# A threshold search over float keys on VectorE, replaced by one over two 16-bit halves on VectorE and ScalarE

## The chip, the cores and the metric

The kernel runs on one core of one Trainium2 chip. The metric is the device time of the whole program in microseconds (us). A core has five engines that work side by side, each on its own queue in order: TensorE (PE in the profile, PEld for its weight loads), VectorE (DVE), ScalarE (ACT), GpSimd (POOL) and SyncE (SP, which issues the DMAs here).

## The reference

One decoder layer over 1,024 tokens of width 1,024: an RWKV-7 mixer and a sparse attention side by side, merged by gates, then a SwiGLU feed-forward network. What matters here is how the sparse attention chooses its keys. An indexer gives each query a score for each earlier key, and the 256 best keys stay:

```python
score = jnp.einsum('bqhs,bqh->bqs', sc, wib) * idx_scale
score = jnp.where(causal, score, -jnp.inf)
_, sel = lax.top_k(score, topk)            # topk = 256
valid = sel <= t[None, :, None]
```

Queries come in eight blocks of 128. Blocks 0 and 1 have at most 256 keys before them and need no choice; block b of 2 to 7 chooses among (b+1) x 128 keys, that is 384 to 1,024. Where scores are equal, the lower index wins. The kernel turns the choice into an additive mask, `bias[b]`: 0 where a key stays, -1e30 where it does not.

## The kernel before

PE works through a list of matmuls in exactly the order in which the program was written; the other engines' queues are ordered by a scheduler at compile time, by program order and by its own idea of when things are ready. What sets PE's order is the pump: `fill` is a queue of generators, and `pump(n)` (L134) takes n matmuls' worth of work from it and puts them into PE's list at that place. So matmuls that depend on nothing urgent (the fill) stand between the steps of a chain that leaves PE free.

The layer's large products are done by `mm3` (L117): weights and activations are each split into a high and a low part, and three products are added, which makes 24 matmuls of 128 x 512 for one column of 128 outputs and one half of the tokens. `weights` (L106) loads a weight tile by SP, ACT copies its high part (L103), DVE subtracts to get the low part (L104). The result in PSUM is emptied by ACT and DVE: L265, L266, L268 and L270 for the rwkv columns, L282 to L286 with L103/L104 or L293/L294 for attention's k and q (rotary embedding), L363 and a transpose (L350, L352) for v, a Tanh on ACT (L376) for the gates.

The order around the change: `norm1` and the indexer's projections; then `fill` is given `proj_rwkv` (14 columns, 672 matmuls) and `proj_qkv` (12 columns, 576 matmuls and some transposes, 1,258 credits with the former), 72 are pumped, and `scores` (L732) computes the indexer scores, 80 pieces with a pump of 2 after each. Then `proj_gates` of half 0 (16 columns, 384 matmuls) joins the queue and `select` (L763) runs. After it the pools of scores and masks' helpers are closed and `rwkv(0)` (L404) runs, in whose fill stand what is left of the gates and then `att0`, the attention of half 0 blended with the other half's gates (748 credits). `rwkv(0)` pumps 806 credits: 403 in each of its two quarters, the first 16 of them ahead of its first matmul (L425, L433). What is still in the queue then runs behind it by `run(*fill)`, before `rwkv(1)` starts.

`select` looks for the 256th largest score of each query bit by bit: in each of 32 steps DVE proposes a bit (L781), counts in each of the six blocks how many scores reach the proposed threshold (L783, one pass with an accumulated sum), compares the count with 256 and keeps the bit or not (L785, L786), and 38 matmuls are pumped. Unsigned integers stand for floats: a mask `mk`, settled after the first step, makes their order that of the scores. The last part (L799 to L810) sets all above the threshold, takes as many ties as are needed by a running sum, and writes the mask.

Of the kernel before, what the change touches and what calls it, by code (L numbers as in the profile page):

```python
# [11 lines left out]
F32 = mybir.dt.float32  # L12
F32R = mybir.dt.float32r
BF16 = mybir.dt.bfloat16
U32 = mybir.dt.uint32
AF = mybir.ActivationFunctionType
ALU = mybir.AluOpType
AX = mybir.AxisListType
# [2 lines left out]
S = 1024  # L21
# [3 lines left out]
TOPK = 256  # L25
C1 = math.exp(-0.5)
NEG = -3.0e38
BIG = 1.0e30
# [17 lines left out]
def block_kernel(ctx: ExitStack, tc: tile.TileContext, ins: dict, outT: bass.AP, stop=None, dbg=None):  # L46
    nc = tc.nc
    V, A, G, T, SY = nc.vector, nc.scalar, nc.gpsimd, nc.tensor, nc.sync
# [47 lines left out]
    def mix():  # L96
        return psM.tile([128, HT], F32, tag="mix", name="mix")
# [33 lines left out]
    fill = deque()  # L131
    credit = [0]

    def pump(n):  # L134

        credit[0] += n
        while credit[0] > 0 and fill:
            try:
                credit[0] -= abs(next(fill[0]))
            except StopIteration:  # L140
                fill.popleft()
        if not fill:
            credit[0] = 0

    def run(*gens):
        for g in gens:
            for _ in g:
                pass
# [31 lines left out]
    def opened(side, name, **kw):  # L180
        stack = ExitStack()
        return stack, stack.enter_context(tc.tile_pool(name=name, bufs=1, side=side, reuse_waits="tile", **kw))
# [59 lines left out]
    def proj(ct, us, out, off=0, between=None):  # L242
        w = weights(ins["w_in"][ct])
        for half, u in enumerate(us):
            if half == 1 and between:
                between()
            ps = acc()
            o = off if half == 0 else 0
            yield from mm3(ps[:, :HT - o], w, u, tok=slice(o, HT))
            out(half, ps)  # L250

    def stage(pool, dt=F32):
        return pool.tile([128, 2, HT], dt, tag="stg", name="stg", bufs=2)

    def proj_rwkv(us, pj):
        for g0, n in ((CT_WA, 1), (CT_GD, 1), (CT_K, 4), (CT_R, 4), (CT_V, 4)):
            for j in range(n):
                ct = g0 + j
                st = stage(pj)
                mu = par[:, P_MU + ct:P_MU + ct + 1]  # L260
                pss = []

                def out(half, ps):
                    s = st[:, half, :]
                    A.activation(s, ps, AF.Copy, scale=omu[:, ct:ct + 1])  # L265
                    V.scalar_tensor_tensor(s[:, 1:], ps[:, :HT - 1], mu, s[:, 1:], op0=ALU.mult, op1=ALU.add)  # L266
                    if half == 0:
                        A.activation(halo[:, ct:ct + 1], ps[:, HT - 1:HT], AF.Copy)  # L268
                    else:
                        V.scalar_tensor_tensor(s[:, 0:1], halo[:, ct:ct + 1], mu, s[:, 0:1],  # L270
                                               op0=ALU.mult, op1=ALU.add)

                yield from proj(ct, us, out)
                SY.dma_start(d_rw[g0][j], st.rearrange("p h t -> p (h t)"))
# [96 lines left out]
    def proj_gates(half, u):  # L371
        for g in range(16):

            def out(_, ps):
                t = tmp()
                A.activation(t, ps, AF.Tanh, scale=0.5)  # L376
                SY.dma_start(d_g[half][g], t)

            yield from proj(CT_GA + g, [u], out)
# [334 lines left out]
    def pieces(n):  # L714

        m = -(-n // 512)
        return [(i * (n // m), n // m) for i in range(m)]
# [11 lines left out]
                V.tensor_scalar(bias[b][:, b * 128:], caus, BIG / 3.0e38, None, op0=ALU.mult)  # L729
        return caus, bias  # L730

    def scores(p, caus):  # L732

        ik = p.tile([128, 2, S], F32R, name="ik")
        for h in range(2):
            for e in range(2):
                SY.dma_start(ik[64 * e:64 * e + 64, :, h * HT:(h + 1) * HT].bitcast(F32),
                             d_ik[h].rearrange("c p t -> p c t"))
        sc = {}
        for b in range(2, 8):  # L740
            n = (b + 1) * 128
            iq = p.tile([128, 8, 128], F32R, tag="iq", name="iq", bufs=2)
            o = (b % 4) * 128
            SY.dma_start(iq.bitcast(F32), d_iq[b // 4][:, :, o:o + 128].rearrange("h p t -> p h t"))
            s = p.tile([128, n], F32, tag=f"sc{b}", name="sc")
            for c, w in pieces(n):
                for h in range(8):
                    ps = mix()
                    for i in range(2):
                        T.matmul(ps[:, :w], iq[:, h, :], ik[:, i, c:c + w], start=i == 0, stop=i == 1)  # L750
                    rl = p.tile([128, 512], F32, tag="rl", name="rl", bufs=3)
                    A.activation(rl[:, :w], ps[:, :w], AF.Relu)
                    if h == 0:
                        V.tensor_scalar(s[:, c:c + w], rl[:, :w], widx[:, b, 0:1], 0.0, op0=ALU.mult, op1=ALU.add)
                    else:
                        V.scalar_tensor_tensor(s[:, c:c + w], rl[:, :w], widx[:, b, h:h + 1], s[:, c:c + w],
                                               op0=ALU.mult, op1=ALU.add)
                    pump(2)
            V.tensor_tensor(s[:, n - 128:n], s[:, n - 128:n], caus, op=ALU.add)
            sc[b] = s  # L760
        return sc

    def select(p, scs, bias):  # L763

        blocks, sc = list(scs), list(scs.values())
        nb, nk = len(blocks), S

        def small(tag, dt=F32):
            return p.tile([128, nb], dt, tag=tag, name=tag)


        Tk = small("Tk", U32)
        V.memset(Tk, 0)
        mk = small("mk", U32)
        V.memset(mk, 0x80000000)
        cnt = small("cnt")
        junk = p.tile([128, nk], BF16, tag="junk", name="junk")
        f = small("f", U32)
        kb = small("kb", U32)
        for bit in range(31, -1, -1):  # L780
            V.scalar_tensor_tensor(f, Tk, 1 << bit, mk, op0=ALU.bitwise_or, op1=ALU.bitwise_xor)  # L781
            for i, s in enumerate(sc):
                V.tensor_scalar(junk[:, :s.shape[1]], s, f.bitcast(F32)[:, i:i + 1], None, op0=ALU.is_ge,  # L783
                                op1=ALU.add, accum_out=cnt[:, i:i + 1])
            V.tensor_scalar(kb, cnt, TOPK - 0.5, float(1 << bit), op0=ALU.is_ge, op1=ALU.mult)  # L785
            V.tensor_tensor(Tk, Tk, kb, op=ALU.bitwise_or)  # L786
            pump(38)
            if bit == 31:

                neg = small("neg")  # L790
                V.tensor_scalar(neg, cnt, TOPK - 0.5, float(0x7fffff00), op0=ALU.is_lt, op1=ALU.mult)
                negu = small("negu", U32)
                V.tensor_copy(negu, neg)
                V.tensor_tensor(mk, mk, negu, op=ALU.bitwise_or)
                V.tensor_scalar(negu, negu, 8, None, op0=ALU.logical_shift_right)
                V.tensor_tensor(mk, mk, negu, op=ALU.bitwise_or)
        V.tensor_tensor(f, Tk, mk, op=ALU.bitwise_xor)
        tau = f.bitcast(F32)
        for i, s in enumerate(sc):  # L799
            n = s.shape[1]  # L800
            t, r = tau[:, i:i + 1], cnt[:, i:i + 1]
            eq = p.tile([128, nk], F32, tag="eq", name="eq")
            V.tensor_scalar(eq[:, :n], s, t, None, op0=ALU.is_equal)
            V.tensor_scalar(junk[:, :n], s, t, None, op0=ALU.is_gt, op1=ALU.add, accum_out=r)
            V.tensor_scalar(r, r, -1.0, TOPK + 0.5, op0=ALU.mult, op1=ALU.add)
            pre = p.tile([128, nk], F32, tag="pre", name="pre")
            V.tensor_tensor_scan(pre[:, :n], eq[:, :n], eq[:, :n], 0.0, op0=ALU.add, op1=ALU.max)
            V.scalar_tensor_tensor(eq[:, :n], pre[:, :n], r, eq[:, :n], op0=ALU.is_le, op1=ALU.mult)
            V.scalar_tensor_tensor(eq[:, :n], s, t, eq[:, :n], op0=ALU.is_gt, op1=ALU.add)
            V.tensor_scalar(bias[blocks[i]], eq[:, :n], BIG, -BIG, op0=ALU.mult, op1=ALU.add)  # L810

    def attend(half, p, bias):
        blocks, nk = blocks_of[half], (half + 1) * HT
# [196 lines left out]
    def chain(*gens):  # L1010
        for g in gens:
            yield from g
# [9 lines left out]
    caus, bias = masks(bp)  # L1022
# [7 lines left out]
    for st, _ in reversed(sx):  # L1030
        st.close()
    ss, sp = opened("right", "se")
    fill.append(chain(proj_rwkv(us, pj), proj_qkv(us, pj, cs)))
    pump(72)
    scs = scores(sp, caus)
    fill.append(proj_gates(0, us[0]))
    select(sp, scs, bias)
    ss.close()
    sc_.close()
    spj.close()  # L1040
# [112 lines left out]
```

## Time and profile before

| what | us |
|---|---|
| median of 3 runs (lowest, highest) | 2025.36 (2018.75, 2028.1) |
| the profiled execution | 2030.08 |
| its span, first to last instruction | 2028.3 |
| PE busy | 1843.1 |
| DVE busy | 1204.7 |
| ACT busy | 736.8 |
| mean granted clock of PE | 0.942 |

The profile shows one execution. "Busy" adds up instructions; PE's matmuls overlap in the pipeline, so their starts say more than their durations. A row of the order in time gives start and duration in us, the engine, the line of the kernel, the operation, and output and input tiles; in brackets stands how long the engine had been idle before it, and what released it. A row by groups gives the count, the summed busy time in us and the mean of one in ns. A row of waits gives the waiting instruction, whom it waited for, us in total, times, and the longest.

### The profile page before, as it was taken

The numbers are of one execution on the slowest core, as the hardware profiler recorded it, in microseconds if no ns is written. First come the engines' busy times: TensorE is split into PE (matmuls) and PEld (weight loads), VectorE is DVE, ScalarE is ACT, GpSimd is POOL, SyncE is SP. The second block draws the span as 40 slices with busy tenths as digits, with TensorE's granted clock in tenths as the row PEclk, the third lists the DMA queues.
The fourth block names the chain that finished last, engine by engine and source line by source line (L and its number), as shares of the span: only waits on it lengthen the run. The fifth ranks groups of instructions, "written<-read, shape, count | busy, mean of one in ns | idle before, by whom it ended". The sixth has DMA issues, their size and how long they took to land. (4 is left out here: it accounts for less than half of the span.)

```text
span 2028.3 us, 26078 instructions
## 1 busy us (share of the span) xinstructions
PE 1843.1 (91%) x10032; PEld 1483.6 (73%) x10032; DVE 1204.7 (59%) x2245; ACT 736.8 (36%) x1220; POOL 37.6 (2%) x22
## 2 busy tenths in 40 slices
PE   3899888778998898989879989999999989999997
PEld 2788666667787676767758868878878868888885
DVE  5679999999264474479477534433347553333334
ACT  4655112452423533533333435542233323222222
POOL 0000000000000000000010000000000000000000
PEclk9899999999997897979869989999999989999998
DMA  4341122332535343246313285414457432533523
GB/s 168 101 133 71 63 75 81 102 122 67 191 104 161 100 115 92 83 137 197 89 51 103 70 218 165 119 50 146 130 174 223 131 116 94 166 105 116 163 84 114
DMA packets 133316, 242.90 MB, mean 120 GB/s; under 512 B 27836, under 2 KB 57152, under 8 KB 133064
## 3 DMA queue, kind: packets, MB, share of 16 engines
q1 hardware_dynamic: 133192, 241.24, 38.9%
q8 instruction: 79, 1.29, 0.3%
q14 instruction: 45, 0.37, 0.1%
HBM read 188.24 MB, written 52.95 MB: 119 GB/s over the span
## 5 line engine op out<-in xcount | busy, mean ns | idle before, releaser
L104 DVE TENSOR_TENSOR wlo<-wst,whi 128x1024 fp32r<-128x1024 f32 (+1 forms) x231 | 278.4, 1206 | 419.4 <-ACT whi L103 229.2
L103 ACT ACTIVATE whi<-wst 128x1024 fp32r<-128x1024 f32 (+1 forms) x231 | 241.2, 1044 | 429.3 <-PE acc L123 394.4
L122 PE MATMUL acc<-zhi,whi 128*128 128x512 f32 x704 | 281.5, 400 | 0.0
L123 PE MATMUL acc<-zlo,whi 128*128 128x512 f32 x704 | 277.6, 394 | 0.0
L783 DVE TENSOR_SCALAR_CACHE_REDUCE junk<-sc,f 128x384 bf16<-128x384 f32 (+2 forms) x192 | 181.4, 945 | 5.5
L122 PE MATMUL acc<-u1hi,whi 128*128 128x512 f32 x376 | 157.9, 420 | 25.0 <-DVE tmp L284 14.0
L127 PE MATMUL acc<-zhi,wlo 128*128 128x512 f32 x704 | 179.2, 394 | 0.0
L122 PE MATMUL acc<-u0hi,whi 128*128 128x512 f32 (+1 forms) x376 | 153.7, 412 | 22.4 <-DVE stg L266 14.8
L122 PEld LDWEIGHTS acc<-zhi,whi 128*128 128x128 f32 x704 | 133.6, 190 | 30.2 <-issue 2.0
L123 PE MATMUL acc<-u1lo,whi 128*128 128x512 f32 x376 | 153.0, 407 | 1.1 <-DVE u1lo L104 0.9
L123 PEld LDWEIGHTS acc<-zlo,whi 128*128 128x128 f32 x704 | 133.6, 190 | 27.8
L127 PEld LDWEIGHTS acc<-zhi,wlo 128*128 128x128 f32 x704 | 130.9, 188 | 29.3 <-issue 1.6
L123 PE MATMUL acc<-u0lo,whi 128*128 128x512 f32 (+1 forms) x376 | 150.7, 404 | 0.9 <-DVE u0lo L104 0.9
L122 PE MATMUL acc<-fhi,whi 128*128 128x512 f32 x352 | 140.5, 399 | 4.1 <-ACT zhi L103 3.9
L123 PE MATMUL acc<-flo,whi 128*128 128x512 f32 x352 | 139.6, 397 | 1.1 <-DVE flo L104 1.1
L122 PEld LDWEIGHTS acc<-u0hi,whi 128*128 128x128 f32 x376 | 75.7, 201 | 45.8 <-DVE stg L266 18.2
L122 PEld LDWEIGHTS acc<-u1hi,whi 128*128 128x128 f32 x376 | 73.7, 196 | 48.3 <-DVE tmp L284 17.5
L127 PE MATMUL acc<-u1hi,wlo 128*128 128x512 f32 x376 | 101.8, 415 | 0.0
L127 PE MATMUL acc<-u0hi,wlo 128*128 128x512 f32 (+1 forms) x376 | 94.5, 394 | 5.4 <-DVE wlo L104 5.4
L127 PE MATMUL acc<-fhi,wlo 128*128 128x512 f32 x352 | 90.6, 396 | 0.0
L123 PEld LDWEIGHTS acc<-u0lo,whi 128*128 128x128 f32 x376 | 75.6, 201 | 17.4 <-DVE u0lo L104 2.5
L127 PEld LDWEIGHTS acc<-u1hi,wlo 128*128 128x128 f32 x376 | 74.4, 201 | 16.5 <-issue 0.3
(223 smaller groups left out, 2887.4 us busy)
## 6 DMA issues: line engine op xcount, KB each, us to landing
wst<-in_w_ffn_in SPq DMA_DIRECT2D x88, 512.0 KB, 3.5
wst<-in_w_in SPq DMA_DIRECT2D x63, 512.0 KB, 3.8
wst<-in_w_fo SPq DMA_DIRECT2D x32, 512.0 KB, 3.6
k<-d_k SPq DMA_DIRECT2D x48, 256.0 KB, 5.4
h<-in_xT SPq DMA_DIRECT2D x32, 256.0 KB, 5.8
d_g<-tmp SPq DMA_DIRECT2D x32, 256.0 KB, 2.2
wst<-in_w_o SPq DMA_DIRECT2D x16, 512.0 KB, 3.5
tmp<-d_g SPq DMA_DIRECT2D x32, 256.0 KB, 3.2
```

The costliest lines, as they stand in the source:

```text
L103: A.activation(hi, x, AF.Copy)
L104: V.tensor_tensor(lo, x, hi.bitcast(F32), op=ALU.subtract)
L122: T.matmul(ps, whi[:, wk + k, :], ahi[:, ak + k, tok], start=k == 0, stop=False)
L123: T.matmul(ps, whi[:, wk + k, :], alo[:, ak + k, tok], start=False, stop=False)
L127: T.matmul(ps, wlo[:, wk + k, :], ahi[:, ak + k, tok], start=False, stop=k == nk - 1)
L783: V.tensor_scalar(junk[:, :s.shape[1]], s, f.bitcast(F32)[:, i:i + 1], None, op0=ALU.is_ge, op1=ALU.add, accum_out=cnt[:, i:i + 1])
```

## The change

The scores are first turned into integers whose order is that of the floats (an arithmetic shift makes a mask of the sign, an xor applies it), and cut into a high half (multiples of 65,536) and a low half (0 to 65,535), each in a tile of its own per block. Two searches of 16 steps follow, the first on the high halves, the second on the low halves of those keys whose high half equals the one found; for this the difference of the high half and the found one is added to the low half, so that all other keys lie out of reach.

In each step the six blocks are counted on two engines: blocks 5, 3 and 2 (768, 512 and 384 keys) by DVE as before, blocks 7, 6 and 4 (1,024, 896 and 640 keys) by ACT, as a sum of `Sign(x + z)`, whose threshold is 2 x 256 - 1 - n. A vector `sgn` of +1 and -1 lets the three small instructions that follow serve both kinds at once. The pumps become 14 after each block's cutting, 18 after each step, 20 between the searches and 22 after each block's mask. The gates of half 0 no longer join the queue before the search: what is left of rwkv and qkv is run out behind it, and only then the gates are queued, for `rwkv(0)`. The scores' tiles stay in one pool, the scoring's other tiles go into a pool that is closed before the search, and the search's tiles take its place.

```diff
-        for bit in range(31, -1, -1):
-            V.scalar_tensor_tensor(f, Tk, 1 << bit, mk, op0=ALU.bitwise_or, op1=ALU.bitwise_xor)
-            for i, s in enumerate(sc):
-                V.tensor_scalar(junk[:, :s.shape[1]], s, f.bitcast(F32)[:, i:i + 1], None, op0=ALU.is_ge,
-                                op1=ALU.add, accum_out=cnt[:, i:i + 1])
-            V.tensor_scalar(kb, cnt, TOPK - 0.5, float(1 << bit), op0=ALU.is_ge, op1=ALU.mult)
-            V.tensor_tensor(Tk, Tk, kb, op=ALU.bitwise_or)
-            pump(38)
...
+        order, nv = [5, 3, 2, 7, 6, 4], 3
...
+            V.tensor_scalar(l, si, 31, 0x7fffffff, op0=ALU.arith_shift_right, op1=ALU.bitwise_and)
+            V.tensor_tensor(l, si, l, op=ALU.bitwise_xor)
+            V.tensor_scalar(h, l, -65536, None, op0=ALU.bitwise_and)
+            V.tensor_scalar(l, l, 65535, None, op0=ALU.bitwise_and)
...
+            pump(14)
...
+        def search(xs, unit):
+            for bit in range(15, -1, -1):
+                for i in list(range(nv, nb)) + list(range(nv)):
+                    x = xs[i]
+                    n = x.shape[1]
+                    if i < nv:
+                        V.tensor_scalar(junk[:, :n], x, z[:, i:i + 1], None, op0=ALU.is_ge, op1=ALU.add,
+                                        accum_out=cnt[:, i:i + 1])
+                    else:
+                        A.activation(junka[:, :n], x, AF.Sign, bias=z[:, i:i + 1], accum_out=cnt[:, i:i + 1])
+                V.tensor_tensor(ge, cnt, thr, op=ALU.is_ge)
+                V.scalar_tensor_tensor(ge, ge, -0.5, sgn, op0=ALU.add, op1=ALU.mult)
+                V.scalar_tensor_tensor(z, ge, unit * float(1 << bit), z, op0=ALU.mult, op1=ALU.add)
+                pump(18)
...
+        search(hi, 65536.0)
...
+            V.scalar_tensor_tensor(lo[i].bitcast(F32), hi[i], top[:, i:i + 1], lo[i],
+                                   op0=ALU.subtract if i < nv else ALU.add, op1=ALU.add)
...
+        pump(20)
+        search([l.bitcast(F32) for l in lo], 1.0)
...
+            pump(22)
...
-    scs = scores(sp, caus)
+    scs = scores(sp, sp1, caus)
+    ss1.close()
+    with tc.tile_pool(name="se2", bufs=1, side="right", reuse_waits="tile") as sp2:
+        select(sp2, scs, bias)
+    run(*fill)
+    fill.clear()
     fill.append(proj_gates(0, us[0]))
-    select(sp, scs, bias)
```

More of the change, by code (lines that the diff above doesn't have):

```diff
@@ L14 @@
 BF16 = mybir.dt.bfloat16
-U32 = mybir.dt.uint32
+I32 = mybir.dt.int32
 AF = mybir.ActivationFunctionType
@@ L730, in masks, with scores @@
         return caus, bias
-    def scores(p, caus):
+    def scores(keep, p, caus):
         ik = p.tile([128, 2, S], F32R, name="ik")
@@ L744, in scores @@
             SY.dma_start(iq.bitcast(F32), d_iq[b // 4][:, :, o:o + 128].rearrange("h p t -> p h t"))
-            s = p.tile([128, n], F32, tag=f"sc{b}", name="sc")
+            s = keep.tile([128, n], F32, tag=f"sc{b}", name="sc")
             for c, w in pieces(n):
@@ L763, in select @@
     def select(p, scs, bias):
-        blocks, sc = list(scs), list(scs.values())
-        nb, nk = len(blocks), S
+        order, nv = [5, 3, 2, 7, 6, 4], 3
+        nb = len(order)
         def small(tag, dt=F32):
             return p.tile([128, nb], dt, tag=tag, name=tag)
[L772 to L778, printed above, removed]
@@ L779, in select @@
-        kb = small("kb", U32)
-        for bit in range(31, -1, -1):
-            V.scalar_tensor_tensor(f, Tk, 1 << bit, mk, op0=ALU.bitwise_or, op1=ALU.bitwise_xor)
-            for i, s in enumerate(sc):
-                V.tensor_scalar(junk[:, :s.shape[1]], s, f.bitcast(F32)[:, i:i + 1], None, op0=ALU.is_ge,
-                                op1=ALU.add, accum_out=cnt[:, i:i + 1])
-            V.tensor_scalar(kb, cnt, TOPK - 0.5, float(1 << bit), op0=ALU.is_ge, op1=ALU.mult)
-            V.tensor_tensor(Tk, Tk, kb, op=ALU.bitwise_or)
-            pump(38)
[L788 to L796, printed above, removed]
@@ L797, in select @@
-        V.tensor_tensor(f, Tk, mk, op=ALU.bitwise_xor)
-        tau = f.bitcast(F32)
-        for i, s in enumerate(sc):
+        hi, lo = [], []
+        for b in order:
+            si = scs[b].bitcast(I32)
+            shape = list(scs[b].shape)
+            h = p.tile(shape, I32, tag=f"hi{b}", name="hi")
+            l = p.tile(shape, I32, tag=f"lo{b}", name="lo")
+            V.tensor_scalar(l, si, 31, 0x7fffffff, op0=ALU.arith_shift_right, op1=ALU.bitwise_and)
+            V.tensor_tensor(l, si, l, op=ALU.bitwise_xor)
+            V.tensor_scalar(h, l, -65536, None, op0=ALU.bitwise_and)
+            V.tensor_scalar(l, l, 65535, None, op0=ALU.bitwise_and)
+            hi.append(h)
+            lo.append(l)
+            pump(14)
@@ new lines, in select @@
+        sgn, thr, cnt, z = small("sgn"), small("thr"), small("cnt"), small("z")
+        V.memset(sgn[:, :nv], 1.0)
+        V.memset(sgn[:, nv:], -1.0)
+        V.memset(thr[:, :nv], TOPK - 0.5)
+        for i in range(nv, nb):
+            V.memset(thr[:, i:i + 1], 2.0 * TOPK - 1.0 - scs[order[i]].shape[1])
+        junk = p.tile([128, S], BF16, tag="junk", name="junk")
+        junka = p.tile([128, S], BF16, tag="junka", name="junka")
+        ge = small("ge")
+        def search(xs, unit):
[12 more added lines that the diff above has]
+                pump(18)
@@ new lines, in select @@
+        V.tensor_scalar(z, sgn, -32768.0, None, op0=ALU.mult)
+        search(hi, 65536.0)
+        top = small("top")
+        V.tensor_copy(top, z)
+        for i in range(nb):
+            V.scalar_tensor_tensor(lo[i].bitcast(F32), hi[i], top[:, i:i + 1], lo[i],
+                                   op0=ALU.subtract if i < nv else ALU.add, op1=ALU.add)
+        V.tensor_scalar(z, sgn, 32767.5, None, op0=ALU.mult)
+        pump(20)
+        search([l.bitcast(F32) for l in lo], 1.0)
+        key, low, msk = small("key", I32), small("low", I32), small("msk", I32)
@@ L800, in select @@
+        V.tensor_tensor(top, top, sgn, op=ALU.mult)
+        V.tensor_tensor(z, z, sgn, op=ALU.mult)
+        V.tensor_copy(key, top)
+        V.tensor_copy(low, z)
+        V.tensor_tensor(key, key, low, op=ALU.bitwise_or)
+        V.tensor_scalar(msk, key, 31, 0x7fffffff, op0=ALU.arith_shift_right, op1=ALU.bitwise_and)
+        V.tensor_tensor(key, key, msk, op=ALU.bitwise_xor)
+        tau = key.bitcast(F32)
+        for i, b in enumerate(order):
+            s = scs[b]
             n = s.shape[1]
@@ L801, in select @@
             t, r = tau[:, i:i + 1], cnt[:, i:i + 1]
-            eq = p.tile([128, nk], F32, tag="eq", name="eq")
-            V.tensor_scalar(eq[:, :n], s, t, None, op0=ALU.is_equal)
+            eq, pre = hi[i].bitcast(F32), lo[i].bitcast(F32)
+            V.tensor_scalar(eq, s, t, None, op0=ALU.is_equal)
             V.tensor_scalar(junk[:, :n], s, t, None, op0=ALU.is_gt, op1=ALU.add, accum_out=r)
             V.tensor_scalar(r, r, -1.0, TOPK + 0.5, op0=ALU.mult, op1=ALU.add)
-            pre = p.tile([128, nk], F32, tag="pre", name="pre")
@@ L807, in select @@
[L807 to L810, printed above, removed]
+            V.tensor_tensor_scan(pre, eq, eq, 0.0, op0=ALU.add, op1=ALU.max)
+            V.scalar_tensor_tensor(eq, pre, r, eq, op0=ALU.is_le, op1=ALU.mult)
@@ L812, in attend @@
+            V.scalar_tensor_tensor(eq, s, t, eq, op0=ALU.is_gt, op1=ALU.add)
+            V.tensor_scalar(bias[b], eq, BIG, -BIG, op0=ALU.mult, op1=ALU.add)
+            pump(22)
     def attend(half, p, bias):
@@ L1032, in block_kernel @@
     ss, sp = opened("right", "se")
+    ss1, sp1 = opened("right", "se1")
     fill.append(chain(proj_rwkv(us, pj), proj_qkv(us, pj, cs)))
     pump(72)
-    scs = scores(sp, caus)
+    scs = scores(sp, sp1, caus)
[4 more added lines that the diff above has]
+    fill.clear()
     fill.append(proj_gates(0, us[0]))
-    select(sp, scs, bias)
     ss.close()
```

## The prediction

> **What bounds the kernel now.** I read the page's totals first, then the busy time in stages, the waits, the order in time around the threshold search, and the groups by shape there.
>
> ```profile
> span 2028.3 us, 26078 instructions
> PE 1843.1 (91%) x10032; PEld 1483.6 (73%) x10032; DVE 1204.7 (59%) x2245; ACT 736.8 (36%) x1220; POOL 37.6 (2%) x22
> ...
> 190.00:326.00 136.00, 114.84 (x458) 89.22 (x458) 130.97 (x307) 20.79 (x36) 0.00 (x0) 0.95 0.22 70
> 326.00:450.00 124.00, 98.45 (x404) 75.30 (x402) 121.38 (x250) 61.06 (x97) 0.00 (x0) 0.99 0.31 106
> 450.00:497.00 47.00, 45.66 (x204) 37.43 (x205) 45.66 (x84) 13.33 (x22) 0.00 (x0) 0.93 0.31 87
> 497.00:547.00 50.00, 44.59 (x183) 35.79 (x182) 18.24 (x18) 16.12 (x25) 0.00 (x0) 0.93 0.57 189
> ...
> 835.00:862.00 27.00, 26.32 (x146) 20.00 (x146) 8.69 (x16) 14.62 (x29) 0.00 (x0) 0.93 0.33 103
> ...
> PE acc L122 <- DVE tmp L284: 20.0, 15, 2.1
> PE acc L122 <- DVE stg L266: 14.8, 8, 2.3
> ```
>
> The stage rows give PE, PEld, DVE, ACT and POOL busy with their counts, then clock, DMA share and GB/s. Over the whole span PE is the bound (91%), and the change leaves its matmuls as they are, so only PE's idle time and slow stretches can be won or lost. From 190 to 450 us, the search, it is the other way round: DVE is busy 252.4 of 260 us and PE issues 862 matmuls, one in 0.30 us. The two waits say on whom PE waits: on DVE emptying its accumulators. ACT has only 82 us of work there.
>
> What PE can do undisturbed shows a little later, in gate columns of 24 matmuls each; beside it, where the stages begin and end:
>
> ```profile
> 526.78 0.60 ACT L376 ACTIVATE tmp<-acc 128x512 f32<-128x512 f32 x1 [0.77 <-PE acc L127]
> ...
> 532.27 0.60 ACT L376 ACTIVATE tmp<-acc 128x512 f32<-128x512 f32 x1 [0.77 <-PE acc L127]
> ...
> 496.25 0.39 PE L122 MATMUL acc<-u0hi,whi 128*128 128x512 f32 x1
> ...
> 503.59 0.69 DVE L810 TENSOR_SCALAR bias<-eq 128x1024 bf16<-128x1024 f32 x1
> ...
> 515.16 0.42 ACT L427 ACTIVATE wa<-wa 64x256 f32<-64x256 f32 x1 [5.26 <-DMA wa<-d_rw]
> ...
> 546.82 0.70 PE L433 MATMUL mix<-wa,wup 64*128 64x256 f32 x2
> ...
> 835.64 0.77 PE L122 MATMUL acc<-u1hi,whi 128*128 128x512 f32 x1
> ...
> 861.65 1.12 PE L884 MATMUL mix<-tmp,ind 2*128 2x512 f32 x2 [0.68 <-ACT tmp L879]
> ```
>
> 24 matmuls in 5.49 us are 0.229 us each. The search ends on DVE at 504.3; PE begins the first gate column, so has finished all of rwkv and qkv, at 496.25; rwkv(0) puts its first matmul on PE at 546.8, behind the ten gate columns queued before it.
>
> **The change, part by part.** One step of the search before, on DVE:
>
> ```profile
> 209.16 0.61 DVE L783 TENSOR_SCALAR_CACHE_REDUCE junk<-sc,f 128x384 bf16<-128x384 f32 x1
> ...
> 209.82 0.75 DVE L783 TENSOR_SCALAR_CACHE_REDUCE junk<-sc,f 128x512 bf16<-128x512 f32 x1
> ...
> 210.60 0.88 DVE L783 TENSOR_SCALAR_CACHE_REDUCE junk<-sc,f 128x640 bf16<-128x640 f32 x1
> ...
> 211.53 1.01 DVE L783 TENSOR_SCALAR_CACHE_REDUCE junk<-sc,f 128x768 bf16<-128x768 f32 x1
> ...
> 212.58 1.15 DVE L783 TENSOR_SCALAR_CACHE_REDUCE junk<-sc,f 128x896 bf16<-128x896 f32 x1
> 213.66 0.74 DVE L266 SCALAR_TENSOR_TENSOR stg<-acc,par,stg 128x511 f32<-128x511 f32 x1
> 214.32 1.27 DVE L783 TENSOR_SCALAR_CACHE_REDUCE junk<-sc,f 128x1024 bf16<-128x1024 f32 x1
> ...
> 215.63 0.17 DVE L785 TENSOR_SCALAR kb<-cnt 128x6 uint32<-128x6 f32 x1
> ...
> 216.24 0.61 DVE L783 TENSOR_SCALAR_CACHE_REDUCE junk<-sc,f 128x384 bf16<-128x384 f32 x1
> ```
>
> *Counts that leave DVE.* From start to start the 640, 896 and 1024 counts take 0.93, 1.08 and 1.31 us, 3.32 together; 32 steps make 106 us less. The three that stay (384, 512, 768) take 0.66 + 0.78 + 1.05 = 2.5 us, the three small instructions 0.61 (215.63 to 216.24), as before: 3.1 us of DVE per step. That the counts read integers I cost at nothing: the operation and width stay, and the rows hold no integer count.
>
> *Passes that come to DVE.* Per block three one-source passes (key mask and two cuts) and two two-source passes (xor, and joining the low half). Nearest rows:
>
> ```profile
> L803 DVE TENSOR_SCALAR eq<-sc,f 128x1024 f32<-128x1024 f32 x1 | 0.8, 754 | 0.0
> ...
> L803 DVE TENSOR_SCALAR eq<-sc,f 128x384 f32<-128x384 f32 x1 | 0.4, 420 | 0.0
> ...
> L809 DVE SCALAR_TENSOR_TENSOR eq<-sc,f,eq 128x1024 f32<-128x1024 f32 x1 | 1.3, 1285 | 0.0
> ...
> L809 DVE SCALAR_TENSOR_TENSOR eq<-sc,f,eq 128x384 f32<-128x384 f32 x1 | 0.6, 615 | 0.0
> ```
>
> Six blocks evenly spaced: six times the mean of first and last, 3.52 us a one-source pass, 5.70 a two-source one; 3 x 3.52 + 2 x 5.70 = 22 us. If the integer one-source passes ran no faster than two-source ones it would be 28.5; less than 22 nothing suggests. The final selection by ties keeps its instructions. The new integer tiles lie where the scoring tiles ik, iq and rl were and so wait for the last score; that costs nothing, since the passes need the scores anyway.
>
> *Counts that come to ACT.* The nearest rows are the softmax exponentials, also with a per-partition bias and an accumulated sum:
>
> ```profile
> L846 ACT ACTIVATE L<-L,mx 128x1024 f32<-128x1024 f32 x8 | 9.2, 1145 | 4.7 <-DVE mx L843 4.7
> ...
> L846 ACT ACTIVATE L<-L,mx 128x896 f32<-128x896 f32 x8 | 8.3, 1042 | 7.6 <-DVE mx L843 7.5
> ...
> L846 ACT ACTIVATE L<-L,mx 128x640 f32<-128x640 f32 x8 | 6.6, 827 | 19.8 <-DVE mx L843 19.8
> ...
> L846 ACT ACTIVATION_READ_ACCUMULATOR L<-L,mx 128x1 f32 x64 | 12.0, 187 | 0.0
> ...
> 632.54 0.40 ACT L846 ACTIVATE L<-L,mx 128x128 f32<-128x128 f32 x1 [3.26 <-DVE mx L843]
> ...
> 632.96 0.40 ACT L846 ACTIVATE L<-L,mx 128x128 f32<-128x128 f32 x1
> ...
> L103 ACT ACT_TABLE_LOAD x1 | 1.3, 1283 | 0.7 <-PEq L1144 0.7
> ```
>
> Durations with their reads: 3.01 + 3 x 0.19 = 3.58 us; the two short ones follow each other in 0.42 instead of 0.59 us, so 0.17 of each pair overlaps: 3.07 us a step, 98 us in all, into an engine that is free for far more than that. But the search becomes a ring over two engines: signs 3.07, small instructions 0.61, two crossings that I estimate at 0.1 each from the gap-free hand-overs: 3.9 us, against 3.1 of DVE work. So DVE waits on ACT for 0.8 us a step, 26 us in 32 steps. Bounds: 0, if fill fits exactly into those waits; and the fill's whole ACT work inside the ring, priced in the rivals. What is queued behind the waiting compare on DVE is the emptying of accumulators, for which PE waits. I take 26 because fill both uses such waits and delays the signs.
>
> The kernel's only table load is the one in the last row (1.3 us, at the start). If Sign needs another table, with only Copy as fill there would be one change in and one out, 2.6 us by that row. The Trainium skill (ScalarE: Activation LUTs, "What ACT_TABLE_LOAD costs" and "Table sets: the hidden batching unit") speaks against mixing functions: about 2.66 us for each change of set with its drain, though copy is in every set. By it the sum below would be 5.3 us higher; the single load row bears out the load's length but not the drain.
>
> *End of the search.* 504.3 - 106 + 22 + 26 = 446 us on DVE, which is no gain by itself: PE must get through rwkv and qkv.
>
> *PE.* The pumps are now 84 + 2 x 288 + 20 + 132 = 812 instead of 1,216, and the rest of qkv is run out behind the search. Of the 1,258 matmuls of rwkv and qkv 232 are issued by the end of scoring, so 1,026 remain at 190 us, before and after. Until 446 I keep the present pace, 0.30 us, since the order of each queue is still set by interleaving fill with search work: (446 - 190) / 0.30 = 853. The other 173 go at 0.229, 40 us, with 2 us for transposes: 488, where 496 was. What PE idles in the stage 497 to 547 (5.4 us, behind the last selections on DVE) I leave out: the gates that met it stand elsewhere now.
>
> *Gates moved behind.* Before, 190 of the 384 gate matmuls were pumped in the search and 16 more at the start of rwkv(0). Now only the latter stand before its first matmul: 24 x 0.229 = 5.5, at 494 instead of 546.8, 53 us earlier. Its inputs come some 11 us behind the search's end (L427 at 515.16, behind 504.3), so they are there. But 190 matmuls more are left over. rwkv(0)'s own pumps total 806 credits; with 194 + 748 of fill some 132 ran after it, and now some 322 do. The present leftover took 26 us (835.6 to 861.6), 0.197 us a credit: 190 cost 37 us; at the gate pace of 0.229, 43.5. With eight gate columns go eight weight loads and eight stores on SP, a split and a Tanh each on ACT and a split on DVE; the leftover's price holds such work already, and from 835 to 862 ACT and DVE are busy for 14.6 and 8.7 of 27 us.
>
> **Sum.** -53 + 37 = -16 us. The profiled execution is 2030.1 us (span 2028.3 and 1.8 around it): 2014. The runs' median is 4.7 lower, so I forecast 2009, 0.8% faster. A difference under 0.5%, 10 us, is about what cannot be told from no change.
>
> **Rivals.** *PE freed earlier.* PE's wait is on DVE, whose work falls by 84 us, so the pace could rise towards 0.229; against it, L284 and L266 stand in fixed places between search instructions. At 0.26, halfway, PE ends at 190 + 267 = 457, rwkv(0) begins at 463, and -84 + 37 = -47: 1978.
>
> *Signs stuck behind fill (slower).* ACT takes its queue in order; a sign waits behind weight splits and rope copies:
>
> ```profile
> L282 ACT ACTIVATE tmp<-acc 32x512 f32<-32x512 f32 x64 | 37.7, 589 | 1.0
> ```
>
> For 18 matmuls the fill is 0.95 us of ACT in rwkv columns, 2.7 in k, 3.2 in q (eight such copies a column, two stagings, one split). With some 19, 11 and 3 steps of each, 55 us all inside the ring: the search ends at 501, PE at 543, rwkv(0) starts at 548.5, +39: 2064. It decides from 0.5 us a step, 16 us in 32, where the gain is gone; half of it gives 2037. For it: the copies come in runs of four. Against: the ring has 0.8 us of ACT free in each step, and DVE's share of fill is already in my sum.
>
> *The engines count one after the other*, because both write columns of one cnt tile: 3.07 + 2.5 + 0.8 = 6.4 a step, 80 us more than 3.9; much the same price as the second, some 2060. Against it speaks
>
> ```profile
> 400.79 1.28 ACT L293 ACTIVATE stg<-tmp 64x512 fp32r<-64x512 f32 x2 [4.25 <-issue]
> ...
> 403.02 1.40 DVE L294 TENSOR_TENSOR stg<-tmp,stg 64x512 fp32r<-64x512 f32 x2
> ```
>
> where ACT writes both its parts of a tile before DVE writes the one that the program puts between.
>
> **How the numbers follow.** Forecast 48%, own range 1999 to 2022 (26 us of waiting more or less at a quarter of its size, since PE then does more beside it; 6 us of tail price; 5 of integer passes or tables). PE freed 22%, down to 1965. Signs behind fill 24%, counts in turn 6%. Range 1972 to 2042, leaving out the extremes of both. Faster by over 0.5%: the 22 and 36 of the 48, 58%. Within: 12 of the forecast and 7 of the mild second rival, 19%. Slower: 23%.
>
> **What would show it.** Right: DVE no longer saturated in the search, its waits released by ACT's signs; steps of 5 to 7 us; search end near 446; first matmul of rwkv(0) near 494; a leftover of some 63 us behind rwkv(0). Wrong: signs with gaps behind L282 or L265; integer passes over 1.3 us at 1024; PE still at 0.30 after the search; a leftover much shorter than 63.

## The result, and the profile after

The changed kernel takes **1973.4 us** (median of 4 runs, 1970.84 to 1976.63) against 2024.2 us for the kernel before (4 runs beside it, 2018.75 to 2028.1): a ratio of **0.9752**, 95% interval 0.9724 to 0.9779, so 2.5% faster. The forecast was 0.8%. 1973.4 us lies 1.4 us inside the lower end of the whole range (1972 to 2042), and outside the forecast's own range (1999 to 2022). The profiled execution took 1976.63 us, 53.5 less than the 2030.08 of the one before; the parts below are worked out between these two.

The totals of the changed kernel's page, to be held against those before:

```profile
span 1974.8 us, 26176 instructions
...
PE 1818.0 (92%) x10032; PEld 1469.1 (74%) x10032; DVE 1118.7 (57%) x2091; ACT 837.7 (42%) x1412; POOL 37.6 (2%) x22
```

DVE lost 86.0 us of work, ACT took over 100.9. PE has as many matmuls as before. The stages of the search follow, in the columns of the stage rows shown in the prediction (mostly: cutting; first search; joining and the first steps of the second search; the rest of the second search; final selection; and what is run out behind it; the limits are rounded, and the first search's counts begin at 207.8, the second's at 287.3):

```profile
190.00:212.00 22.00, 22.00 (x98) 18.04 (x97) 20.84 (x47) 7.61 (x14) 0.00 (x0) 1.00 0.29 96
212.00:282.00 70.00, 70.00 (x307) 57.46 (x306) 60.28 (x167) 61.64 (x116) 0.00 (x0) 1.00 0.27 93
282.00:316.00 34.00, 33.61 (x147) 27.23 (x145) 28.84 (x68) 28.20 (x50) 0.00 (x0) 1.00 0.32 109
316.00:391.00 75.00, 60.08 (x241) 47.07 (x242) 65.14 (x152) 72.45 (x128) 0.00 (x0) 0.95 0.29 104
391.00:431.00 40.00, 16.83 (x64) 13.28 (x63) 39.64 (x66) 10.28 (x18) 0.00 (x0) 0.70 0.14 53
431.00:474.00 43.00, 42.75 (x203) 34.87 (x201) 9.42 (x13) 18.40 (x30) 0.00 (x0) 1.00 0.56 173
```

In the first search PE is busy all the time, 307 matmuls in 70 us: one in 0.228 us, the pace that the prediction had measured in the gate columns, where the kernel before needed 0.30. DVE now has 10 of 70 us free. From 316 us on, in the second search among the k and q columns, PE falls back to 75 / 241 = 0.31 us, the pace that it had there in the kernel before (124 / 404 = 0.307), while ACT is busy 72.45 of 75 us. So the faster pace stands almost wholly in the rwkv columns. In the final selection PE does next to nothing. The waits of PE between 190 and 475 us say on whom:

```profile
PE acc L122 <- DVE tmp L284: 38.5, 8, 23.2
```

The order in time shows where (PE's rows, with two of DVE's between them):

```profile
395.82 0.86 PE L127 MATMUL acc<-u1hi,wlo 128*128 128x512 f32 x3
...
419.03 0.68 DVE L284 SCALAR_TENSOR_TENSOR tmp<-acc,cs 128x512 f32<-128x512 f32 x1
...
419.86 0.76 PE L122 MATMUL acc<-u0hi,whi 128*128 128x512 f32 x1 [23.17 <-DVE tmp L284]
...
430.08 0.49 DVE L844 TENSOR_SCALAR bias<-hi 128x640 bf16<-128x640 f32 x1
...
470.20 0.48 PE L122 MATMUL acc<-u0hi,whi 128*128 128x512 f32 x1
...
474.05 0.70 PE L433 MATMUL mix<-wa,wup 64*128 64x256 f32 x2
...
802.32 0.70 PE L433 MATMUL mix<-wa,wup 64*128 64x256 f32 x2
```

The 14.8 us of waits on L266, the emptying of the rwkv columns, are gone, and so is every wait on L268 (8.6 us before). What is left is, but for 0.2 us, one kind, and more than half of it is a single hole of 23.17 us: the rotary step that empties a q column (L284) ran at 419.03, in the middle of the final selection, which ended at 430.6. rwkv(0) begins at 474.05 (before 546.82), rwkv(1) at 802.32 (before 862.70).

One step of the first search in the order of time, DVE first:

```profile
217.65 1.01 DVE L803 TENSOR_SCALAR_CACHE_REDUCE junk<-hi,z 128x768 bf16<-128x768 int32 x1
...
218.59 0.75 DVE L266 SCALAR_TENSOR_TENSOR stg<-acc,par,stg 128x511 f32<-128x511 f32 x1
219.25 0.74 DVE L803 TENSOR_SCALAR_CACHE_REDUCE junk<-hi,z 128x512 bf16<-128x512 int32 x1
...
221.11 0.17 DVE L807 TENSOR_TENSOR ge<-cnt,thr 128x6 f32<-128x6 f32 x1 [0.45 <-ACT junka L806]
```

And ACT:

```profile
217.71 1.15 ACT L806 ACTIVATE junka<-hi,z 128x1024 bf16<-128x1024 int32 x1
...
218.99 1.04 ACT L806 ACTIVATE junka<-hi,z 128x896 bf16<-128x896 int32 x1
...
220.03 0.15 ACT L268 ACTIVATE halo<-acc 128x1 f32<-128x1 f32 x1
220.16 0.83 ACT L806 ACTIVATE junka<-hi,z 128x640 bf16<-128x640 int32 x1
```

Both engines start at 217.7, so they count at the same time; the rwkv column's emptying (L266, L268) fits between their passes; DVE's compare waits 0.45 us for the last sign.

Behind the search, the two quarters of rwkv(0) (up to where L433 and then the last L637 stand) and the leftover after them. Before:

```profile
547.00:698.00 151.00, 136.41 (x976) 110.24 (x975) 79.77 (x175) 55.86 (x108) 7.03 (x3) 0.86 0.41 119
698.00:835.00 137.00, 118.55 (x989) 93.67 (x988) 77.34 (x188) 58.17 (x131) 6.48 (x3) 0.85 0.33 94
```

After, with the leftover as the third row:

```profile
474.00:615.00 141.00, 138.07 (x1014) 111.86 (x1014) 79.89 (x158) 54.02 (x91) 7.04 (x3) 0.95 0.40 118
615.00:744.00 129.00, 113.28 (x955) 90.03 (x954) 76.80 (x190) 58.47 (x127) 6.49 (x3) 0.89 0.47 128
744.00:802.00 58.00, 57.32 (x335) 43.57 (x333) 18.70 (x40) 29.83 (x65) 0.00 (x0) 0.98 0.38 121
```

The first quarter is 10 us shorter though it issues 38 matmuls more: PE idles 2.9 us in it instead of 14.6, and the granted clock is 0.95 instead of 0.86. The second is 8 us shorter. The leftover grew from 27 to 58 us. **Where the 53.5 us come from:** start of rwkv(0) -72.8, its quarters -18.5 (the rows are rounded at their edges), the leftover +31, and +7 behind rwkv(1)'s start. The last is not explained; in the experiments below that stretch was 1 to 8 us longer than in the profiled execution before.

### The profile page after: what moved, and what is told of

Read it like the earlier page. It is cut to its first block, busy times and chain, and to the rows that moved or that the text cites. A ratio compares the mean times of both kernels' runs of the same rounds, so it can differ in the third digit from the quotient of the medians.

```text
span 1974.8 us, 26176 instructions
## 1 busy us (share of the span) xinstructions
PE 1818.0 (92%) x10032; PEld 1469.1 (74%) x10032; DVE 1118.7 (57%) x2091; ACT 837.7 (42%) x1412; POOL 37.6 (2%) x22
## 5 line engine op out<-in xcount | busy, mean ns | idle before, releaser
L104 DVE TENSOR_TENSOR wlo<-wst,whi 128x1024 fp32r<-128x1024 f32 (+1 forms) x231 | 278.4, 1205 | 451.1 <-ACT whi L103 234.3
L122 PE MATMUL acc<-u1hi,whi 128*128 128x512 f32 x376 | 153.5, 408 | 5.0 <-DVE tmp L284 3.4
L878 DVE CUSTOM_DVE_ANT_0 L<-mix,bias 128x384 f32<-128x384 f32 (+5 forms) x64 | 34.4, 538 | 95.6 <-PE mix L876 95.4
L123 PEld LDWEIGHTS acc<-u1lo,whi 128*128 128x128 f32 x376 | 72.4, 193 | 16.8 <-DVE u1lo L104 2.5
```

Of the source, the lines that this page charges most:

```text
L104: V.tensor_tensor(lo, x, hi.bitcast(F32), op=ALU.subtract)
L122: T.matmul(ps, whi[:, wk + k, :], ahi[:, ak + k, tok], start=k == 0, stop=False)
L123: T.matmul(ps, whi[:, wk + k, :], alo[:, ak + k, tok], start=False, stop=False)
L878: V.tensor_tensor_reduce(L[:, c:c + w], ps[:, :w], bias[b][:, c:c + w], -1.0, last, ALU.add, ALU.min, mx[:, ci:ci + 1])
```

## The experiments

Two theories stand at the start. **Relief:** what counts is that DVE has room, so that accumulators are emptied when they are full and PE runs at its own pace. **Order:** what counts is the other half of the change, the gates moved behind the search and the shorter pumps, and the counting engine matters little. The experiments show that neither holds alone. Ratios are to the kernel before, run beside each group.

**All six counts on DVE.** Halves, pumps and gates stay as changed; only the engine goes back.

```diff
-        order, nv = [5, 3, 2, 7, 6, 4], 3
+        order, nv = [5, 3, 2, 7, 6, 4], 6
...
-        V.memset(sgn[:, nv:], -1.0)
```

> The changed kernel with all six blocks counted by DVE; halves, pumps and the late gates as changed. If the gain comes from the counts that left DVE (relief of DVE): DVE is saturated again in the search, PE falls back from 0.225 to about 0.30 us a matmul in the first search, the search ends near 520 us, and the time is 2015 to 2045. If it comes from the later gates and the new pumps: PE keeps its pace or rwkv(0) starts early all the same, and the time stays under 1990.

Measured: 2022.16 us, ratio 0.9975 (0.9959 to 0.9991). A stretch of the search and the one before rwkv(0):

```profile
190.00:290.00 100.00, 89.45 (x373) 71.37 (x372) 97.21 (x222) 17.54 (x29) 0.00 (x0) 0.97 0.21 74
...
490.00:512.00 22.00, 0.25 (x1) 0.25 (x2) 22.00 (x37) 2.26 (x4) 0.00 (x0) 0.50 0.47 145
```

Its waits of PE from 190 to 520 us:

```profile
PE mix L433 <- ACT wa L427: 28.8, 1, 28.8
...
PE acc L122 <- DVE stg L266: 15.7, 6, 3.4
```

DVE is full again, PE issues 373 matmuls in 100 us (438 in the same stretch of the changed kernel), that is 0.27 us each and not the 0.30 expected, the waits on L266 are back, and at the end PE waits for rwkv(0)'s inputs while DVE is still choosing. So with the rest as changed the move to ACT is worth 2022 - 1973 = 49 us (45 by the two ratios), nearly the whole gain. The relief of DVE is its cause, but not through PE's pace alone: rwkv(0) begins at 511.75, 37.7 us later than in the changed kernel, and of these PE's fill accounts for only 8.9; the other 28.8 are the wait in the first row, for a search that takes longer when DVE does all of it. (The changed kernel's hole of 23 us hides part of what the pace is worth.)

**Gates late alone**, in the kernel before:

```diff
     scs = scores(sp, caus)
-    fill.append(proj_gates(0, us[0]))
     select(sp, scs, bias)
+    run(*fill)
+    fill.clear()
+    fill.append(proj_gates(0, us[0]))
```

> The kernel before with one edit: the gates of half 0 are queued behind the search, as in the change. Relief of DVE: PE at 0.30 in the search as before, rwkv(0) starts some 25 us earlier, its quarters get shorter and what is left over behind it longer by about as much, 2005 to 2025. Gates and pumps: most of the gain is here, under 1990.

Measured: 2016.11 us, ratio 0.9946 (0.993 to 0.9961), 0.5% faster. PE's pace in the search is that of before (344 matmuls from 190 to 290 us); then it waits for rwkv(0)'s inputs:

```profile
PE mix L433 <- ACT wa L427: 18.7, 1, 18.7
```

The two quarters and the leftover:

```profile
513.00:657.00 144.00, 140.72 (x1014) 113.06 (x1014) 80.73 (x160) 55.98 (x97) 6.50 (x3) 0.92 0.39 123
657.00:786.00 129.00, 113.53 (x957) 90.78 (x957) 76.47 (x189) 58.65 (x128) 6.49 (x3) 0.89 0.45 128
786.00:844.00 58.00, 57.32 (x333) 43.23 (x333) 18.56 (x40) 29.68 (x66) 0.00 (x0) 0.99 0.38 121
```

rwkv(0) begins 33.6 us earlier (25 were expected) and the leftover is as long as in the changed kernel, 31 us longer than before: those two nearly cancel. What remains is the quarters, 7 and 8 us shorter, with the clock at 0.92 and 0.89 instead of 0.86 and 0.85. So the quarters' gain belongs to the moved gates. In this order of the steps the gates' move (about -12) and the halves with the new pumps (2022 - 2016, about +6) together are a small part; the rest is the relief of DVE. The shares are not fixed sizes: with pumps of 30 the gates' move is worth 26 us (last run below), and the relief with the gates left ahead of the search and pumps of 18 was not run. The wait of 18.7 us also says what the relief is made of: PE's fill ends here at 494.5, in the changed kernel 20 us earlier, and there the wait for the search is gone, another 19.

**More pump per step.** If DVE and ACT have room, more fill can go into the steps, and the last q columns no longer meet the final selection.

```diff
-                pump(18)
+                pump(24)
```

> The changed kernel with a pump of 24 instead of 18 after each step, nothing else. If PE's hole of 23 us behind the search (395 to 419) comes from q columns that stand later in the program than the final selection and so yield to it on DVE, the hole shrinks and the time falls by 10 to 20, to 1953 to 1963. If the hole comes from DVE's work as such, it moves, and the time stays within 6 of 1973.

Measured: **1951.05 us**, ratio 0.9633 (0.9597 to 0.9668), a little below the 1953 to 1963 expected. The hole is gone; of PE's waits on L284 from 190 to 520 us this is left, and rwkv(0) begins at 448.8:

```profile
PE acc L122 <- DVE tmp L284: 9.4, 7, 2.4
```

The selection ends at 444.8, 14 us later than in the changed kernel, and the time falls nevertheless: in the changed kernel the end of the search is not what sets the time. The hole is not all of it. In the second search, where the changed kernel issued 241 matmuls, this run and the one with a pump of 30 (below) issue 278 and 305:

```profile
316.00:391.00 75.00, 68.03 (x278) 53.43 (x277) 65.41 (x145) 72.07 (x125) 0.00 (x0) 0.95 0.34 120
316.00:391.00 75.00, 70.99 (x305) 56.48 (x305) 64.56 (x133) 70.98 (x122) 0.00 (x0) 1.00 0.38 130
```

DVE and ACT are as busy as with 18 (65.14 and 72.45 us). So here PE's pace, 0.31, 0.27 and 0.25 us, is set by how much fill the program puts between two steps, and not by DVE's room.

**Each sign count of the first search done twice**, the second time into a vector that nobody reads: work is added and nothing left out.

```diff
                         A.activation(junka[:, :n], x, AF.Sign, bias=z[:, i:i + 1], accum_out=cnt[:, i:i + 1])
+                        if unit > 1.0:
+                            A.activation(junka[:, :n], x, AF.Sign, bias=z[:, i:i + 1], accum_out=cnx[:, i:i + 1])
```

> The changed kernel with every sign count of the first search done twice, the second into a vector that nobody reads: 16 x 3.07 = 49 us more of ACT in the ring, nothing more on DVE. If PE's pace hangs on DVE's load, PE stays at 0.225 to 0.24 in the first search, the search ends some 45 us later, and the time rises by 5 to 20 at most. If the gain is the shorter search itself, it rises by 40 to 50, to about 2020.

Measured: 1990.69 us, ratio 0.9828 (0.9797 to 0.9859).

```profile
190.00:290.00 100.00, 100.00 (x438) 82.07 (x437) 66.14 (x157) 83.61 (x155) 0.00 (x0) 1.00 0.27 95
290.00:390.00 100.00, 82.62 (x321) 64.94 (x320) 72.90 (x162) 93.98 (x168) 0.00 (x0) 0.90 0.26 95
...
475.39 1.22 PE L433 MATMUL mix<-wa,wup 64*128 64x256 f32 x2 [6.94 <-ACT wa L427]
...
493.00 0.79 PE L433 MATMUL mix<-wa,wup 64*128 64x256 f32 x1 [9.40 <-ACT x L435]
```

(Two stretches, then two matmuls of PE's order in time.) The selection ends at 490.5, 60 us later (45 were expected), and the kernel loses 17. A step of the first search takes 9.2 us here (16 in the 147.5 us from 207.1 to 354.6) and 7.6 in the run with all counts on DVE (207.1 to 328.0), with the same pump of 18; yet PE runs at its full pace here, where DVE is busy 66 of 100 us, and not there, where it is 97. So in the first search the pace hangs on DVE's room, and not on the fill per step. The 17 us appear at the start of rwkv(0), where PE is done with its fill and now waits for inputs: the chain of the search, hidden in the changed kernel, is what is late next. (The hole of 23 us is not in this run either, since the q columns are done before the final selection: PE's fill ends 5.6 us earlier than in the changed kernel, and then the waits begin.)

**What makes the hole.** In program order six pumps of 22 stand between the masks, and the last q column ends at credit 1056 of 1,258, of which 912 are pumped by the end of the steps. First all 132 ahead of the final selection:

```diff
         tau = key.bitcast(F32)
+        pump(132)
...
             V.tensor_scalar(bias[b], eq, BIG, -BIG, op0=ALU.mult, op1=ALU.add)
-            pump(22)
```

> The changed kernel with its six pumps of 22 (one behind each block's mask) put together into one pump of 132 ahead of the final selection; the search keeps its pumps of 18. If the hole of 23 us is q columns that yield on DVE to selections that stand ahead of them in the program, these columns now go first: the hole shrinks below 5 us and the time falls by 10 to 22, to 1951 to 1963, near that with pumps of 24. If the pump of 24 helped by feeding PE more during the search itself, this gives 1968 to 1978.

Measured: 1971.03 us, ratio 0.9731 (0.9704 to 0.9758): no gain beside the changed kernel's 0.9752 (0.9724 to 0.9779). The hole stands, a little shorter:

```profile
433.09 0.80 PE L122 MATMUL acc<-u1hi,whi 128*128 128x512 f32 x1 [18.35 <-DVE tmp L284]
```

The expectation was missed, but 912 + 132 = 1044: the copies of the last q column still stood behind the selection. With 150 in place of 132:

> One number is changed against the kernel with 132 credits ahead of the final selection: 150. With 912 credits up to there, 132 reach credit 1044, and the last q column ends only at 1056, so its rope copies still stood behind the final selection on DVE and PE's hole stayed (18.35 us at 414.7 us). If it is the place of the last q column's copies against the final selection that makes the hole, 150 (credit 1062) removes it: no wait of the accumulators on L284 above 5 us between 390 and 470, rwkv(0)'s first matmul some 15 to 18 us earlier than the 474 of the changed kernel, and 1953 to 1960 us in all. If the hole comes from the final selection's own work on DVE, wherever the copies stand, the hole stays at 15 to 20 us and the time at some 1971.

Measured: 1961.64 us, ratio 0.9662 (0.9619 to 0.9704). No hole is left among PE's waits on L284:

```profile
PE acc L122 <- DVE tmp L284: 14.4, 8, 2.6
```

rwkv(0) begins at 456.0, 18 us earlier than in the changed kernel, as expected (15 to 18), and 14.1 earlier than with 132. A wait of 6.25 us on the copy of a v column (L363, ACT) has come in, and the time is a little above the 1953 to 1960 expected. The intervals of the two ratios meet at 0.9704, so the time alone would settle little; the profile does. It is the copies' place behind the final selection on DVE's queue that makes the hole.

**Pump 30**, to see whether more fill still pays:

```diff
-                pump(18)
+                pump(30)
```

> The changed kernel with a pump of 30 instead of 18. If only the program order of q columns and final selection matters, 24 did it all, and 30 gives the same within 6 us, 1946 to 1958. If feeding PE earlier goes on to help, it falls below 1944; if the fill now gets in the way of the search's small instructions, it rises above 1960.

Measured: 1949.97 us, ratio 0.9631 (0.9605 to 0.9657), the same as with 24. PE now arrives too early:

```profile
449.50 0.79 PE L433 MATMUL mix<-wa,wup 64*128 64x256 f32 x1 [13.97 <-ACT wa L427]
```

The selection ends at 448.3, and PE waits at rwkv(0)'s inputs as in the runs where the search was late. From here on the search's chain is the bound.

**Gates back into the search**, in the kernel with pump 30, whose 14 us of wait they could fill:

```diff
+    fill.append(proj_gates(0, us[0]))
     with tc.tile_pool(name="se2", bufs=1, side="right", reuse_waits="tile") as sp2:
         select(sp2, scs, bias)
-    run(*fill)
-    fill.clear()
-    fill.append(proj_gates(0, us[0]))
```

> As with pumps of 30, but the gates of half 0 join the queue before the search, as in the kernel before, so that about 170 of their 384 matmuls and their Tanh on ACT stand in the search. If late gates help because rwkv(0)'s first quarter with pure gates as fill has less idle PE and a higher clock, this one is slower by 5 to 15. If early gates only fill the start of rwkv(0) and shorten what is left behind it, it is the same or faster by up to 10. If Tanh and Sign need different tables, loads of 1.3 us each appear on ACT, and it is slower by 15 or more.

Measured: 1976.22 us, ratio 0.9738 (0.9691 to 0.9785): 26 us slower than pump 30, where 5 to 15 were expected.

```profile
479.00:636.00 157.00, 139.71 (x979) 112.87 (x977) 80.35 (x172) 54.94 (x106) 7.08 (x3) 0.85 0.38 115
636.00:775.00 139.00, 122.11 (x980) 96.34 (x980) 77.63 (x191) 58.74 (x131) 7.94 (x3) 0.83 0.31 93
```

rwkv(0) begins 30 us later, its leftover falls from 58 to 29, and its quarters grow by 13 and 8 us, with the clock at 0.85 and 0.83. That is the effect of the run with the gates late alone with the opposite sign, and larger; why it is larger stays open. A change of tables is not the reason: this run too has a single table load.

## Why the prediction was right and wrong

Right in direction and in the prices of the search's work, and the time lies just inside the range; but the gain was 51 us instead of the 16 forecast, because two steps on PE's side failed. Step by step:

- **Counts and passes.** The prices held:

```profile
L806 ACT ACTIVATE junka<-hi,z 128x1024 bf16<-128x1024 int32 x16 | 18.4, 1147 | 7.2 <-DVE z L809 6.5 <-DVE z L812 0.3
L806 ACT ACTIVATE junka<-hi,z 128x896 bf16<-128x896 int32 x16 | 16.6, 1038 | 0.3
L806 ACT ACTIVATE junka<-hi,z 128x640 bf16<-128x640 int32 x16 | 13.2, 824 | 0.2
...
L103 ACT ACT_TABLE_LOAD x1 | 1.3, 1283 | 0.7 <-PEq L1184 0.7
...
L803 DVE TENSOR_SCALAR_CACHE_REDUCE junk<-hi,z 128x768 bf16<-128x768 int32 x16 | 16.2, 1012 | 0.5
...
L807 DVE TENSOR_TENSOR ge<-cnt,thr 128x6 f32<-128x6 f32 x32 | 5.2, 164 | 8.2 <-ACT junka L806 7.6
...
L781 DVE TENSOR_TENSOR lo<-sc,lo 128x1024 int32<-128x1024 int32 x1 | 1.2, 1212 | 0.0
L780 DVE TENSOR_SCALAR lo<-sc 128x1024 int32<-128x1024 int32 x1 | 0.7, 681 | 0.0
```

  A sign costs what an exponential did, an integer count what a float count did, and the integer passes a little less than their neighbours among the float ones. There is one table load in the whole program, as before, so the 2.6 us for tables were rightly left out; the estimate of 5.3 us by the Trainium skill (ScalarE: Activation LUTs, "What ACT_TABLE_LOAD costs") did not come up, since Sign did not change the table here. What its drain would cost, no run here shows.
- **End of the search: 446 forecast, 430.6 measured.** From 190 us to the search's end, the kernel before:

```profile
190.00:504.30 314.30, 262.03 (x1076) 204.14 (x1075) 305.10 (x648) 96.63 (x154) 0.00 (x0) 0.96 0.26 85
```

  and the changed one:

```profile
190.00:430.60 240.60, 202.12 (x850) 162.76 (x849) 214.35 (x496) 179.80 (x321) 0.00 (x0) 0.94 0.26 92
```

  DVE is busy 305.1 of 314.3 us before and 214.4 of 240.6 after. So its work fell by 91 us; 9 of these are fill that now comes later, and the search's own work fell by 82 (84 forecast). Its waiting grew by 17 (26 forecast), of which only 7.6 us stand at the compare behind ACT's signs; 11.9 stand at fill that waits for ACT (L104 for a weight split, L266 for a copy). The rival of signs stuck behind fill is there in small: ACT is busy 72 of 75 us in the second search, whose 16 steps take 104 us (287.8 to 391.7) against 74 for the first. How much of these 30 us is signs behind copies the runs do not separate. The price was paid by the search's chain, which had slack: rwkv(0)'s first input was ready at 444.86 (L427), 29 us before PE came to it.
- **The step that failed: "Until 446 I keep the present pace, 0.30 us".** The reason given was that each queue's order is still set by interleaving. In the first search that was wrong: the cause there was that DVE had no room, and with room PE went at 0.228. In the second search the pace did stay at 0.31, and the reason held too: with DVE and ACT as busy as with 18, pumps of 24 and 30 alone raised 241 matmuls to 278 and 305. At 0.30 PE would have issued 802 of its 1,026 matmuls by 430.6; it issued 850, although it stood still for 23 us of that time. Without the hole the pace is 217.4 / 850 = 0.256. That this is about the halfway value of the rival of PE freed earlier is luck: it is the mean of a stretch at full pace and one at the old pace, and the rival had neither the split nor the hole. The matmuls behind the search, short transposes among them, went at 43 / 203 = 0.212. PE was done with qkv at 470.2 instead of 488, and rwkv(0) began at 474.05 instead of 494. The rival had 463 and 1978 us; the run gave 474 and 1973.
- **The second step that failed: the tail, +37.** The leftover's size was right in kind (58 us, forecast 63; +31). But the prediction let the quarters of rwkv(0) be as long as before, and they lost 18 us. With gate columns in the place of the attention that they push back, PE idles less in them, and the granted clock is higher. The net of the two was +13 instead of +37.
- **Gates in front of rwkv(0)** were the 16 matmuls of its first pump: in PE's order a `u0` column begins at 470.20, and L433 follows at 474.05, 3.85 us later. The prediction named the 16 and priced a whole column of 24, 5.5 us.

Of the 37 us by which the profiled gain exceeded the sum, about 20 come from PE's pace and 24 from the tail; the 7 us behind rwkv(1)'s start go the other way.

## What to carry to other kernels

Where an engine that empties accumulators is as full as here (97% busy in the search), take the pace that PE shows where nothing holds it as the most that its relief can give. Ask for each stretch whether room or the order of the queue holds PE: here it was room in the rwkv columns, the order in the k and q columns. Then look for the next place where the emptying stands behind a long run of other work in its queue, as here behind the final selection. When work is moved off that engine, set anew how much fill goes with each step: 24 instead of 18 gave another 22 us and, with 30, the best times of all (about 1950 us, 3.7% under the kernel before). And price moved fill at its new place too: gate columns between the steps of rwkv(0) shortened its two quarters by 15 to 21 us.

## What the hardware showed that was not expected

The granted clock went with how densely PE was fed, in the same code: 0.86 in a quarter of rwkv(0) with 14.6 us of idle PE, 0.95 with 2.9 us, 0.85 with 17.3 us in the run with the gates back in the search; and 0.70 in the 40 us that held the hole. So an idle stretch goes with a second loss, in the clock around it. By the Trainium skill (TensorE: Matmul & The Clock Gate, "Part 1: The HAM clock gate") the clock is throttled by default and activity releases it, so the idle time would come first. The trace agrees at the hole: matmuls start 0.23 us apart right ahead of it (394.19, 394.42), 0.43 apart behind it (420.84, 421.27), and 0.23 apart again from 425.0 on. For the short gaps inside rwkv(0) no run here separates the two. ScalarE took int32 tiles straight into Sign with a bias and an accumulated sum at the price of float tiles: 1147 ns for 128x1024 as integers in the first search; in the second, on floats, 1149.
